# Operand loads, weight-sum stores, splits and norms of a feed-forward stage moved between queues and engines

## The chip, the cores and the metric

The kernel runs on one core of one Trainium2 chip. The metric is the device time of one launch in microseconds (us), the median of several runs. The core has five engines with an instruction queue each: TensorE (PE) multiplies matrices, VectorE (DVE) and GpSimd (POOL) work element by element, ScalarE (ACT) copies and evaluates functions, SyncE (SP) only issues DMAs. POOL and ACT can issue DMAs as well. Every queue is worked off in order.

## The reference

One layer of a diffusion backbone, on 128 context tokens and 2048 latent tokens of width 1024, all in float32:

```python
h = rmsnorm(x, norm1_g) * (1 + scale1) + shift1
z = h @ w_in                       # columns go to three groups A, B, C
mix = concat(A: gated linear attention, B: conv module, C: gMLP) @ w_out
x = x + gate1 * mix
h = rmsnorm(x, norm2_g) * (1 + scale2) + shift2
x = x + gate2 * (square(relu(h @ w_ff1)) @ w_ff2)      # 1024 -> 4096 -> 1024
y = rmsnorm(x, final_g)
```

Context and latent tokens have modulations of their own. The change touches the last four lines only.

## The kernel before, in words

Tokens stand in 17 tiles of 128 (tile 0 is the context). A float32 operand is split into a high part, rounded to the PE's float32r (ScalarE's copy), and a low part, the rest (a subtraction on DVE or POOL); each product is then three matmuls (mm3, L179): high x high, high x low, low x high. A "split" below is that copy and that subtraction.

The stages run one after another: attention, convolution and gating (to L1161), out_proj for tiles 16 down to 0 (L784, the loop at L1181), FF1 (loop at L1419), FF2 (loop at L1555). Both FF stages multiply 2 x 2 blocks by a Strassen-like scheme of seven products p = 0..6, whose operands are sums of blocks. The latent tokens make two groups g of 1024.

FF1: for each group, 16 iterations i over 256 columns of w_ff1. An iteration has 28 units on PE (seven products of four units, 12 matmuls a product), and in group 0 eight more for the context tile (ff1_context, L1307). Right operands (the tokens' sums, seven products of two halves) are made in out_proj (h2_pair, L835), stored to tb_d, and loaded and split by right_operand (L1173) once for a group: while out_proj and the first iteration run for group 0, and in the last iteration of group 0 for group 1. They lie in T tiles (18) and u tiles (12); the left operands, the weights, in v tiles (11), with left_operand (L1211) preparing the next iteration's in eight steps. `after(p)` (L1269) takes each product out of PSUM into fx, fy and fz, squares, combines and stores them to f_d as right operands of FF2.

FF2: eight chunks c of 512 hidden columns, four blocks b of four token tiles; a block has 28 units of three matmuls and two units of the context tile, 90 matmuls. Operands are loaded by w2_operand, f_operand and fc_operand into o tiles (24), T tiles and s tiles, and split in split_two (L1386), by DVE and POOL in turn. DVE adds each product to the output tiles ya (L1498); the residual x1 is loaded into these first (residual, L1465). The sums of w_ff2's blocks for chunk c + 1 are made in blocks 0 and 1 of chunk c by w2_prep (L1346): load, multiply by the gate and store three, then four combinations and store four, all on POOL. In the last chunk the tiles are normed (norm, L1477) and stored by SP.

What sets the order: `weave` (L154) puts a list of items (position, function) between PE's units, and PE's own instructions stay in program order. DMAs issued with ld_in_order (L136) stay in program order on SP's queue. The order of the rest on each engine is chosen when the kernel is built, by a planner that goes by its own costs; on the chip each queue then runs in that order. A tile of a pool with n buffers is written when the earlier one in its place was read for the last time.

Of the kernel before, what the change touches and what calls it, by code (L numbers as in the profile page):

```python
# [8 lines left out]
F32 = mybir.dt.float32  # L9
# [34 lines left out]
def tile_hybrid(  # L44
# [713 lines left out]

    staged = {}

# [23 lines left out]
    def out_proj(t):  # L784
# [9 lines left out]
        def done(half):  # L794
            def f(pz):
                fs = slice(half * 512, (half + 1) * 512)
                V.tensor_tensor(out=tmp[:, fs], in0=pz, in1=g1rows[cd][:, fs], op=ALU.mult)
                V.tensor_tensor(out=x1[:, fs], in0=tmp[:, fs], in1=x1[:, fs], op=ALU.add)
                if half == 1:
                    st.dma_start(out=x1_d[t], in_=x1)  # L800
                    ssq = const.tile([P, 1], F32, name="ssq3", bufs=2)
                    act(tmp, x1, AF.Square, accum_out=ssq)
                    rstd_of(ssq, ssq, D)
                    S.mul(tmp, x1, ssq)
            return f
# [367 lines left out]
    def right_operand(g, i, kk, dst):  # L1173

        unit = tunit if i < 4 else uunit
        hi, lo = unit(), unit()
        st.dma_start(out=lo.bitcast(F32).rearrange("p (k n) -> p k n", k=2), in_=tb_d[g][:, i, 2 * kk:2 * kk + 2])
        split_in_place(hi, lo, G if kk else V)
        dst[i, kk] = (hi, lo)
# [23 lines left out]
    def wunit(dt=F32R):  # L1203
        return fp.tile([P, D], dt, tag="v", name="v", bufs=11)

# [44 lines left out]
    def ff1_units(g, i, w, tb):  # L1250
# [4 lines left out]
        fx = xf.tile([P, 2, 512], F32, tag="fx", name="fx", bufs=2)  # L1255
        fy = xf.tile([P, 2, 512], F32, tag="fy", name="fy", bufs=1)
        fz = xf.tile([P, 3, 512], F32, tag="fz", name="fz", bufs=1)
# [11 lines left out]
        def after(p):  # L1269
            if p == 0:  # L1270
                S.copy(out=f00, in_=za)
            elif p == 1:
                V.tensor_tensor(out=f00, in0=f00, in1=gb, op=ALU.add)
                square(f00)
            elif p == 2:
                S.copy(out=f01, in_=za)  # L1276
            elif p == 3:
                S.copy(out=fy[:, 0], in_=zc)
            elif p == 4:
                V.tensor_tensor(out=f11, in0=fy[:, 0], in1=za, op=ALU.add)  # L1280
                square(f11)
            elif p == 5:
                V.tensor_tensor(out=f01, in0=f01, in1=zc, op=ALU.add)
                square(f01)
                comb(fz[:, 0], f00, f01, ALU.subtract)
                comb(fy[:, 1], f01, f11, ALU.add)
                comb(fy[:, 0], fy[:, 1], f00, ALU.subtract)
                st.dma_start(out=dst[:, 2:4], in_=fy)
            else:
                act(f10, za, AF.Relu)  # L1290
                V.tensor_tensor(out=f10, in0=f10, in1=f10, op=ALU.mult)
                comb(fz[:, 1], f10, fy[:, 0], ALU.subtract)
                st.dma_start(out=dst[:, 0:2], in_=fx)
                st.dma_start(out=dst[:, 4:7], in_=fz)
# [47 lines left out]
    for i, kk in ORDER[8:]:  # L1342
        right_operand(0, i, kk, TB[0])
    turn = None

    def w2_prep(i, unit, g2):  # L1346
# [10 lines left out]
        def gate():  # L1357
            for x in box:
                G.tensor_tensor(out=x, in0=x, in1=g2, op=ALU.mult)
            st.dma_start(out=d_[:, 0], in_=box[0][:, 0:512])  # L1360
            for f, p in ((0, 1), (1, 5)):
                st.dma_start(out=d_[:, p], in_=box[1][:, f * 512:f * 512 + 512])

        def step():
# [5 lines left out]
            for p, o in ((2, x), (4, y), (3, w), (6, z)):  # L1370
                st.dma_start(out=d_[:, p], in_=o)

# [12 lines left out]

    def split_two(hi, lo, src):  # L1386
        ctr[0] += 1
        S.copy(out=hi, in_=src)  # L1388
        (G if ctr[0] % 2 else V).tensor_tensor(out=lo, in0=src, in1=hi.bitcast(F32), op=ALU.subtract)  # L1389

    def operand(src, unit):

        hi, lo = unit(), unit()
        lv = lo.bitcast(F32)
        ld_in_order(out=lv.rearrange("p (a n) -> p a n", a=src.shape[1]), in_=src)
        split_two(hi, lo, lv)
        return hi, lo

    def w2_operand(c, p, out, unit=ounit):
        x = operand(w2_d[c][:, :, p], unit)  # L1400
        for q in range(CP):
            out[p, q] = [y[:, q * 512:(q + 1) * 512] for y in x]

    def f_operand(c, b, n, out, unit=ounit):
# [3 lines left out]
        s = f_d[c][g][:, ps, :, ts].rearrange("p a q n -> p (a q) n")  # L1408
        x = operand(s, unit if n < 3 else sunit)
        for a in range(s.shape[1]):  # L1410
            out[2 * n + a // 2, a % 2] = [y[:, a * 256:a * 256 + 256] for y in x]

    def fc_operand(c, out):
        x = operand(fc_d[c].rearrange("p q f n -> p (q f) n"), sunit)
        for q in range(2):
# [3 lines left out]
    for g in range(2):  # L1419
        for i in range(NP):  # L1420
            units = ff1_units(g, i, w, TB[g])
            items = []
            if g == 0:
                more, nxt_turn = ff1_context(i, w)
                units = units + more
                if turn is not None:
                    items.append((5, turn))
                turn = nxt_turn
            elif i == 0:
                items.append((5, turn))  # L1430
            if (g, i) == (0, 0):
                items += [(12, late3[0][1]), (20, late3[1][1])]
            if (g, i) != (1, NP - 1):
                w, steps = left_operand((i + 1) % NP)
                items += zip((0, 0.5, 5.5, 10.5, 13.5, 17.5, 18.5, 25.5), steps)
            if (g, i) == (1, NP - 1):

                items += [(x, lambda n=n: f_operand(0, 0, n, F, tunit)) for x, n in ((5, 0), (9, 1), (15, 2))]
                items.append((11, lambda: w2_operand(0, 0, w2, tunit)))
            if g == 1 and i == 3:  # L1440
# [18 lines left out]
    left, right = slice(0, 512), slice(512, 1024)  # L1459

    def tiles_of(b):

        return [NT - 1 - 8 * (b // 2) - 4 * (b % 2) - 2 * j for j in range(2)]

    def residual(b):  # L1465

        for t in sum([[e, e - 1] for e in tiles_of(b)], []):
            ya[t] = tunit(F32)
            ld_in_order(out=ya[t], in_=x1_d[t])

# [15 lines left out]
    def ff2_units(c, b, F, w2):  # L1486
# [19 lines left out]
        def unit(p, j, q):  # L1506
# [9 lines left out]
            if q == CP - 1:  # L1516
                after(p, j)

        return [lambda p=p, j=j, q=q: unit(p, j, q) for p in range(7) for j in range(2) for q in range(CP)]

# [3 lines left out]
    def context(c, b, Fc):  # L1524
# [3 lines left out]
        def load():  # L1528
# [3 lines left out]
            box.extend([ounit(), ounit()])  # L1532
            split_two(*box, rw)

# [13 lines left out]
    w2_operand(0, 1, w2)  # L1548
    residual(0)
    for p in range(2, 7):  # L1550
# [4 lines left out]
    for c in range(NC_):  # L1555
# [7 lines left out]
        for b in range(4):  # L1563
# [18 lines left out]
            if b == 0 and c > 0:  # L1582
                items += wl(c, (0.5, 5), (5, 6), w2)
            if c == 0 and b < 3:
                items.append((8, lambda: residual(b + 1)))
            if b in (0, 1) and more:
                items += zip((6, 12, 26), w2_prep(CP * (c + 1) + b, raw, g2r))
            weave(units, items)
# [34 lines left out]
```

## Time and profile before

| | us |
|---|---|
| runs | 2476.52, 2482.58, 2478.18 (median 2478.18) |
| profiled execution | 2481.85 |
| its span, first to last instruction | 2480.1 |

| engine | busy us | instructions |
|---|---|---|
| PE | 2270.2 | 12018 |
| DVE | 1818.1 | 2624 |
| ACT | 980.4 | 1788 |
| POOL | 1216.4 | 1087 |

The profiled execution is one run of the program with the hardware profiler on; its times are taken in us from the start of its span. A matmul's end is modelled, so a busy PE can still be slower than it could be. Where the profile names what ended an engine's idle time ("<-ACT v L176"), it is inferred from semaphores: the engine, the tile that it wrote, the line of the kernel.

### The profile page before, as it was taken

To read this page: it belongs to the slowest core of one execution; us is meant where nothing else is said; L and a number is where in the kernel's file an instruction comes from. 1 tells how busy PE (TensorE), PEld (TensorE's weight loads), DVE (VectorE), ACT (ScalarE), POOL (GpSimd) and SP (SyncE) were. 2 spreads that over 40 slices of the span, in tenths; PEclk is the share of its full clock that TensorE was granted. 3 is DMA by queue.
4 is the path that set the end of the run, shared out by engine and by line. 5 is a ranking of instruction groups with operands and counts; after the bars stand their busy time and mean duration, and the time that the engine had idled before them with its cause. 6 is when DMAs were issued, how large, how long until landed. Compare 5 with 4: busy or idle time off the path is not lost. (4 is left out here: it accounts for less than half of the span.)

```text
span 2480.1 us, 33032 instructions
## 1 busy us (share of the span) xinstructions
PE 2270.2 (92%) x12018; PEld 1852.5 (75%) x12018; DVE 1818.1 (73%) x2624; ACT 980.4 (40%) x1788; POOL 1216.4 (49%) x1087
## 2 busy tenths in 40 slices
PE   7999999999988987799999699899799999999996
PEld 5788886777767766588888477687587778778775
DVE  5887855877887865587777677776577777877577
ACT  4666664333344455333333332233332233233243
POOL 2332325444423445344334554644956866776742
PEclk9999999999989999899999799999899999999998
DMA  8655635333445456543444454545965666567564
GB/s 284 229 197 195 225 103 177 121 126 125 130 155 191 155 172 206 170 134 126 131 147 155 159 173 154 177 158 179 350 227 195 234 213 228 198 215 234 183 220 149
DMA packets 221764, 452.68 MB, mean 183 GB/s; under 512 B 17973, under 2 KB 118623, under 8 KB 218016
## 3 DMA queue, kind: packets, MB, share of 16 engines
q1 hardware_dynamic: 171456, 263.57, 32.4%
q0 software_dynamic: 50144, 186.99, 21.5%
q8 instruction: 95, 1.56, 0.3%
q14 instruction: 69, 0.57, 0.1%
HBM read 285.07 MB, written 165.43 MB: 182 GB/s over the span
## 5 line engine op out<-in xcount | busy, mean ns | idle before, releaser
L131 PE MATMUL z<-w,hb 128*128 128x512 f32 (+1 forms) x2486 | 558.4, 371 | 14.6 <-ACT hb L776 8.7
L131 PEld LDWEIGHTS z<-w,hb 128*128 128x128 f32 x2486 | 420.3, 191 | 90.5 <-ACT hb L776 8.9
L1388 ACT CAST o<-o 128x1024 fp32r<-128x1024 f32 x148 | 155.6, 1051 | 433.1 <-DMA o<-f_d 297.3
L131 PE MATMUL z<-T,v 128*128 128x512 f32 x1152 | 284.3, 400 | 33.0 <-ACT v L176 10.5
L131 PE MATMUL z<-u,v 128*128 128x512 f32 x1152 | 282.8, 404 | 31.9 <-ACT fy L1276 15.0
L131 PEld LDWEIGHTS z<-u,v 128*128 128x128 f32 x1152 | 223.2, 195 | 87.9 <-ACT fy L1276 20.3
L131 PE MATMUL z<-o 128*128 128x512 f32 x1080 | 265.4, 393 | 20.9 <-DVE T L1498 20.8
L131 PEld LDWEIGHTS z<-T,v 128*128 128x128 f32 x1152 | 220.1, 193 | 83.8 <-ACT v L176 10.7
L131 PE MATMUL g<-o 128*128 128x512 f32 x1116 | 269.6, 391 | 0.0
L131 PEld LDWEIGHTS z<-o 128*128 128x128 f32 x1080 | 201.2, 188 | 72.1 <-DVE T L1498 28.2
L1267 POOL TENSOR_TENSOR fz<-fx,fy 128x512 f32<-128x512 f32 x64 | 99.4, 1554 | 294.2 <-DVE fy L67 293.1
L131 PEld LDWEIGHTS g<-o 128*128 128x128 f32 x1116 | 210.6, 189 | 44.1
L1498 DVE TENSOR_TENSOR T<-T,z 128x512 f32<-128x512 f32 x256 | 171.7, 682 | 96.4 <-PE z L131 95.8
L67 DVE SCALAR_TENSOR_TENSOR cacc<-xp,wd,cacc 128x512 f32<-128x512 f32 (+2 forms) x360 | 237.5, 713 | 0.0
L1389 POOL TENSOR_TENSOR o<-o 128x1024 fp32r<-128x1024 f32 x71 | 177.1, 2503 | 120.3 <-ACT o L1388 119.9
L131 PE MATMUL z<-w,T 128*128 128x512 f32 x720 | 182.0, 407 | 7.0 <-ACT T L776 3.6
L1389 DVE TENSOR_TENSOR o<-o 128x1024 fp32r<-128x1024 f32 x77 | 159.9, 2078 | 26.0 <-ACT o L1388 17.8
L1498 DVE TENSOR_TENSOR T<-T,g 128x512 f32<-128x512 f32 x192 | 129.3, 683 | 67.3 <-PE g L131 66.8
L131 PE MATMUL z<-o,s 128*128 128x512 f32 x576 | 150.3, 405 | 23.2 <-DVE o L1389 19.7
L131 PEld LDWEIGHTS z<-w,T 128*128 128x128 f32 x720 | 137.0, 195 | 36.0 <-POOL T L777 4.5
L177 DVE TENSOR_TENSOR v<-raw,v 128x1024 fp32r<-128x1024 f32 x64 | 131.1, 2050 | 29.5 <-PE z L131 28.1
L131 PEld LDWEIGHTS z<-o,s 128*128 128x128 f32 x576 | 112.1, 196 | 50.6 <-DVE o L1389 22.2
(320 smaller groups left out, 3710.7 us busy)
## 6 DMA issues: line engine op xcount, KB each, us to landing
raw<-in_w_ff_dram SPq DMA_DIRECT2D x124, 512.0 KB
o<-f_d SPq DMA_DIRECT2D x93, 512.0 KB
o<-w_d SPq DMA_DIRECT2D x55, 512.0 KB
w_d<-raw POOLq DMA_DIRECT2D x98, 256.0 KB, 4.5
f_d<-fz POOLq DMA_DIRECT2D x32, 768.0 KB, 5.6
raw<-in_w_mod_dram SPq DMA_DIRECT2D x32, 512.0 KB
f_d<-fy POOLq DMA_DIRECT2D x32, 512.0 KB, 4.0
f_d<-fx POOLq DMA_DIRECT2D x32, 512.0 KB, 4.7
```

The source lines that it names most:

```text
L67: return V.scalar_tensor_tensor(out=out, in0=in0, scalar=scalar, in1=in1, op0=op0, op1=op1)
L131: tc.keep_in_program_order(T.matmul(out, lhsT, rhs, start=start, stop=stop, skip_group_check=read))
L177: order(V.tensor_tensor(out=lo, in0=src, in1=hi.bitcast(F32), op=ALU.subtract))
L1267: G.tensor_tensor(out=out, in0=a, in1=b, op=op)
L1388: S.copy(out=hi, in_=src)
L1389: (G if ctr[0] % 2 else V).tensor_tensor(out=lo, in0=src, in1=hi.bitcast(F32), op=ALU.subtract)
L1498: V.tensor_tensor(out=y, in0=y, in1=bank, op=ALU.add)
```

## The change

1. right_operand's loads are issued by SP in program order (they were POOL's).
2. The context tile's norm before FF1 is taken out of out_proj(0): it runs at unit 2.5 of FF1's first iteration, its scaling on DVE and not on ACT; the two halves that use it move from units 12 and 20 to 16 and 23.
3. In FF1 fy has two buffers and v tiles are 10; the sum f01 + f11 is DVE's (it was POOL's) and the two halves of fy change places, which f_operand undoes.
4. In group 0, from the second iteration on, the context units come first and the left operand's eight steps 8 units later.
5. w2_prep's stores are issued by ACT (they were POOL's). Its tiles in FF2 are T tiles (they were raw), and its items stand 4 units earlier.
6. split_two is told its engine: in chunk 0 all w2 splits are DVE's, later those of products 1, 3, 5, 6; of the f operands only the second (n = 1) is POOL's, except in the very first block; the context weights' are DVE's in blocks 0 and 1, POOL's in 2 and 3.
7. residual(0) and residual(1) are loaded in the last iteration of FF1 (units 19 and 25).
8. The last block of the last chunk runs all products of its first token pair and then those of the second.

```diff
@@ -756,7 +756,7 @@
-    staged = {}
+    staged, last_norm = {}, []
@@ -799,9 +799,17 @@
-                    act(tmp, x1, AF.Square, accum_out=ssq)
-                    rstd_of(ssq, ssq, D)
-                    S.mul(tmp, x1, ssq)
+                    def normed(scale):
+                        act(tmp, x1, AF.Square, accum_out=ssq)
+                        rstd_of(ssq, ssq, D)
+                        scale(tmp, x1, ssq)
+                    if t == 0:
+                        last_norm.append(lambda: normed(lambda o, i, m: V.tensor_scalar(o, i, m, None, op0=ALU.mult)))
+                    else:
+                        normed(S.mul)
@@ -1174,7 +1182,7 @@
-        st.dma_start(out=lo.bitcast(F32).rearrange("p (k n) -> p k n", k=2), in_=tb_d[g][:, i, 2 * kk:2 * kk + 2])
+        ld_in_order(out=lo.bitcast(F32).rearrange("p (k n) -> p k n", k=2), in_=tb_d[g][:, i, 2 * kk:2 * kk + 2])
@@ -1201,7 +1209,7 @@
-        return fp.tile([P, D], dt, tag="v", name="v", bufs=11)
+        return fp.tile([P, D], dt, tag="v", name="v", bufs=10)
@@ -1253,7 +1261,7 @@
-        fy = xf.tile([P, 2, 512], F32, tag="fy", name="fy", bufs=1)
+        fy = xf.tile([P, 2, 512], F32, tag="fy", name="fy", bufs=2)
@@ -1282,14 +1290,14 @@
+                V.tensor_tensor(out=fy[:, 0], in0=f01, in1=f11, op=ALU.add)
-                comb(fy[:, 1], f01, f11, ALU.add)
-                comb(fy[:, 0], fy[:, 1], f00, ALU.subtract)
+                comb(fy[:, 1], fy[:, 0], f00, ALU.subtract)
-                comb(fz[:, 1], f10, fy[:, 0], ALU.subtract)
+                comb(fz[:, 1], f10, fy[:, 1], ALU.subtract)
@@ -1341,6 +1349,16 @@
+    def tiles_of(b):
+        return [NT - 1 - 8 * (b // 2) - 4 * (b % 2) - 2 * j for j in range(2)]
+    def residual(b):
+        for t in sum([[e, e - 1] for e in tiles_of(b)], []):
+            ya[t] = tunit(F32)
+            ld_in_order(out=ya[t], in_=x1_d[t])
@@ -1357,9 +1375,9 @@
-            st.dma_start(out=d_[:, 0], in_=box[0][:, 0:512])
+            S.dma_start(out=d_[:, 0], in_=box[0][:, 0:512])
-                st.dma_start(out=d_[:, p], in_=box[1][:, f * 512:f * 512 + 512])
+                S.dma_start(out=d_[:, p], in_=box[1][:, f * 512:f * 512 + 512])
@@ -1368,7 +1386,7 @@
-                st.dma_start(out=d_[:, p], in_=o)
+                S.dma_start(out=d_[:, p], in_=o)
@@ -1383,21 +1401,20 @@
-    def split_two(hi, lo, src):
-        ctr[0] += 1
+    def split_two(hi, lo, src, eng):
-        (G if ctr[0] % 2 else V).tensor_tensor(out=lo, in0=src, in1=hi.bitcast(F32), op=ALU.subtract)
-    def operand(src, unit):
+        eng.tensor_tensor(out=lo, in0=src, in1=hi.bitcast(F32), op=ALU.subtract)
+    def operand(src, unit, eng):
-        split_two(hi, lo, lv)
+        split_two(hi, lo, lv, eng)
-        x = operand(w2_d[c][:, :, p], unit)
+        x = operand(w2_d[c][:, :, p], unit, V if c == 0 or p in (1, 3, 5, 6) else G)
@@ -1406,12 +1423,12 @@
-        x = operand(s, unit if n < 3 else sunit)
+        x = operand(s, unit if n < 3 else sunit, G if n == 1 and c + b else V)
-            out[2 * n + a // 2, a % 2] = [y[:, a * 256:a * 256 + 256] for y in x]
+            out[3 - a // 2 if n == 1 else 2 * n + a // 2, a % 2] = [y[:, a * 256:a * 256 + 256] for y in x]
-        x = operand(fc_d[c].rearrange("p q f n -> p (q f) n"), sunit)
+        x = operand(fc_d[c].rearrange("p q f n -> p (q f) n"), sunit, V)
@@ -1422,21 +1439,23 @@
-                units = units + more
+                units = more + units if i else units + more
-                    items.append((5, turn))
+                    items.append((8.5 if i else 5, turn))
-                items += [(12, late3[0][1]), (20, late3[1][1])]
+                items += [(2.5, last_norm[0]), (16, late3[0][1]), (23, late3[1][1])]
-                items += zip((0, 0.5, 5.5, 10.5, 13.5, 17.5, 18.5, 25.5), steps)
+                o_ = 8 if g == 0 and i else 0
+                items += [(x + o_, f) for x, f in zip((0, 0.5, 5.5, 10.5, 13.5, 17.5, 18.5, 25.5), steps)]
-                items.append((11, lambda: w2_operand(0, 0, w2, tunit)))
+                items += [(11, lambda: w2_operand(0, 0, w2, tunit)), (19, lambda: residual(0)), (25, lambda: residual(1))]
@@ -1457,16 +1476,6 @@
-    def tiles_of(b):
-        return [NT - 1 - 8 * (b // 2) - 4 * (b % 2) - 2 * j for j in range(2)]
-    def residual(b):
-        for t in sum([[e, e - 1] for e in tiles_of(b)], []):
-            ya[t] = tunit(F32)
-            ld_in_order(out=ya[t], in_=x1_d[t])
@@ -1516,6 +1525,8 @@
+        if last and b == 3:
+            return [lambda p=p, j=j, q=q: unit(p, j, q) for j in range(2) for p in range(7) for q in range(CP)]
@@ -1530,7 +1541,7 @@
-            split_two(*box, rw)
+            split_two(*box, rw, G if b > 1 else V)
@@ -1546,7 +1557,6 @@
-    residual(0)
@@ -1581,10 +1591,10 @@
-            if c == 0 and b < 3:
+            if c == 0 and 0 < b < 3:
-                items += zip((6, 12, 26), w2_prep(CP * (c + 1) + b, raw, g2r))
+                items += zip((2, 8, 22), w2_prep(CP * (c + 1) + b, lambda: tunit(F32), g2r))
```

## Rows read from the trace of the kernel before

**Rows 1.** The page's first part: busy us, share of the span, instructions.
```profile
PE 2270.2 (92%) x12018; PEld 1852.5 (75%) x12018; DVE 1818.1 (73%) x2624; ACT 980.4 (40%) x1788; POOL 1216.4 (49%) x1087
```

**Rows 2.** Stretches: us, PE PEld DVE ACT POOL busy, PE's granted clock, DMA share, GB/s.
```profile
979.50:1037.90 58.40, 32.27 (x122) 23.96 (x121) 36.21 (x38) 28.97 (x42) 27.99 (x25) 0.82 0.49 158
1037.90:1348.70 310.80, 310.80 (x1542) 263.32 (x1541) 238.71 (x225) 99.87 (x140) 127.77 (x109) 1.00 0.42 135
...
1375.40:1423.90 48.50, 28.57 (x88) 19.67 (x87) 34.37 (x28) 17.01 (x21) 29.52 (x22) 0.72 0.43 144
1423.90:1737.20 313.30, 296.19 (x1262) 240.20 (x1261) 235.10 (x215) 92.55 (x119) 164.07 (x134) 0.97 0.49 168
1737.20:1779.50 42.30, 26.07 (x92) 19.96 (x91) 19.66 (x19) 14.81 (x16) 38.17 (x29) 0.80 0.98 357
1779.50:2465.60 686.10, 649.93 (x2791) 526.37 (x2789) 512.00 (x596) 218.01 (x268) 442.04 (x284) 0.99 0.63 213
2465.60:2480.10 14.50, 0.01 (x1) 0.00 (x0) 7.12 (x17) 1.61 (x6) 2.17 (x4) 0.61 0.43 158
...
2444.90:2465.60 20.70, 20.70 (x90) 16.81 (x90) 19.30 (x38) 7.77 (x20) 2.65 (x5) 1.00 0.41 144
```

**Rows 3.** The switch of groups: loads on POOL, ACT's copy, landing times, DMA share.
```profile
1370.35 0.53 POOL L1177 DMA_DIRECT2D T<-tb_d  x1
...
1386.46 0.57 POOL L1177 DMA_DIRECT2D T<-tb_d  x1
...
1409.45 0.54 POOL L1177 DMA_DIRECT2D u<-tb_d  x1
...
1402.86 1.04 ACT L1170 CAST T<-T 128x1024 fp32r<-128x1024 f32 x1
...
DMA to landing us min/median/max: 3.9/6.1/9.1
...
1380.00:1385.00 5.00, 2.27 (x10) 1.50 (x8) 5.00 (x2) 0.90 (x2) 5.00 (x3) 1.00 0.00 0
```

**Rows 4.** FF2's splits by engine: ns min/median/max of one, first and last start.
```profile
L1389 DVE TENSOR_TENSOR o<-o x77: 1210/1366/5761, 1752.4 to 2443.0; 128x1024 fp32r<-128x1024 f32 x77
L1389 POOL TENSOR_TENSOR o<-o x71: 2359/2408/3374, 1744.2 to 2439.9; 128x1024 fp32r<-128x1024 f32 x71
```

**Rows 5.** FF1's start, timeline: start us, us, engine, [idle before it, ended by].
```profile
988.30 1.15 ACT L804 ACTIVATE raw<-w,ssq 128x1024 f32<-128x1024 f32 x1 [3.90 <-POOL ssq L166]
...
974.84 1.11 POOL L1177 DMA_DIRECT2D T<-tb_d  x2
...
1022.70 0.57 POOL L1177 DMA_DIRECT2D u<-tb_d  x1
...
990.44 5.04 PE L131 MATMUL z<-T,v 128*128 128x512 f32 x12 [10.46 <-ACT v L176]
...
1032.24 2.50 PE L131 MATMUL z<-u,v 128*128 128x512 f32 x5 [4.14 <-POOL u L1171]
```

**Rows 6.** PE's waits, 1425 to 1737: us in total, times, longest.
```profile
PE z L131 <- ACT fy L1276: 12.7, 4, 6.6
PE z L131 <- DVE fz L1280: 4.3, 2, 2.2
```

**Rows 7.** Stores of weight sums on POOL: ns min/median/max of one issue.
```profile
L1371 POOL DMA_DIRECT2D w_d<-raw x56: 542/560/569, 1766.5 to 2337.1; - x56
```

**Rows 8.** FF2's first block: PE's waits (1737 to 1780), SP's residual loads.
```profile
PE z L131 <- DVE o L1389: 9.8, 2, 8.3
PE g L131 <- POOL o L1389: 6.4, 1, 6.4
...
1730.12 2.08 SPq L137 DMA_DIRECT2D T<-x_d  x4
```

**Rows 9.** PE's waits in FF2 after that, 1779.5 to 2444.
```profile
PE z L131 <- DVE T L1498: 23.7, 19, 3.2
PE z L131 <- DVE o L1389: 11.4, 5, 2.3
```

**Rows 10.** ACT's waits, 1779 to 2440.
```profile
ACT o L1388 <- DMA o<-f_d: 283.1, 69, 17.1
```

## The prediction

> **What bounds the kernel now.** The page's first part comes first: TensorE (PE) is busy for 92% of the span, DVE for 73% [rows 1]. A busy PE is not a PE at its rate, so the stage table is next [rows 2]. The window 2444.9 to 2465.6 is one block of FF2 without a gap: 90 matmuls in 20.7 us, 0.23 us each. Fourteen iterations of group 0 of FF1 take 310.8 us, 22.2 each; an iteration of group 1 has 84 matmuls of the same kind, 84 x 0.23 = 19.3 us. Against these rates each stage has lost:
>
> - start of FF1: 58.4 - 22.2 = 36.2 us
> - switch to group 1: 48.5 - 19.3 = 29.2 us
> - the other 15 iterations of group 1: 313.3 - 15 x 19.3 = 23.8 us
> - first block of FF2: 42.3 - 20.7 = 21.6 us
> - the other 31 blocks: 686.1 - 31 x 20.7 = 44.4 us
> - after the last matmul: 14.5 us.
>
> That is 169.7 us in places where PE waits, part of it at the lower granted clock (the mean is 0.72 in the switch, so some of it ran at 1.2 GHz and not 2.4). Steady group 0 loses nothing (84 x 0.23 + 24 matmuls of half the width is 22.1). For each place the waits and timelines then say what ended last.
>
> **The change part by part.**
>
> *Right operands on SP's queue.* At the switch PE waits for splits of the operands just loaded. The loads sit in POOL's queue: one is issued at 1370.4, the next at 1386.5, the last at 1409.4, while one takes 3.9 to 9.1 us to land, and in 1380 to 1385 the DMA engines are idle (share 0.00) [rows 3]. So POOL's combinations and splits delay the issue. On SP nothing computes ahead of the loads. What is queued behind them there are two w_ff1 loads per iteration. A right operand's place is free when its product p is done, and it is wanted again one iteration later, 19.3 less 2.8 us of its own product. Landing (6.1) + ACT's copy (1.0) + split on POOL (2.4 [rows 4]) + a second load of the same product behind it (about 1.5) = 11 us; it fits into 16.5, but ACT, DVE and POOL have 14 copies and splits beside an iteration's own work, and the context product now stands ahead of the others and frees the places 2.9 us later. I leave 7 of the 29.2 us: gain **22**. Bounds: 8 (only 14 issues of 0.57 us leave POOL's queue) and 27 (2 us left).
>
> In a sentence of its own: the Trainium skill (DMA: Bandwidth & Descriptors, section "Issuing engines are not separate DMA queues") says that transfers started by any engine share the same 16 engines and that another issuing engine saves only issuing time, usually small. By that rule the gain here would be the lower bound, 8; the idle DMA engines in [rows 3] speak against it, since the issue itself is what comes late.
>
> *Start of FF1; last norm deferred.* PE's first wait is 10.46 us on ACT's copy of the weights. ACT had before it the context tile's scaling at 988.3, which had waited 3.9 us for POOL's power [rows 5]. The change takes this scaling out of ACT and runs it on DVE at unit 2.5; nobody wants it until unit 16. Then loads trickle, from 974.8 to 1022.7, and PE's last wait is for a split at 1032.2 [rows 5]. On SP they go when their places come free; those of products 4 to 6 lie in memory that out_proj's weights hold until about 979.5, product 3 waits for tiles of the last token pair. I expect PE to start about 4 us earlier and the iteration to end 12 us earlier on top: gain **16** of 36.2. Bounds 5 (half of the first wait) and 27 (the first wait and most of the later ones).
>
> *fy doubled, one combination on DVE, stores of weight sums off POOL.* In the rest of group 1 PE waits 12.7 us on ACT's copy into fy, which waits for fy's store, and 4.3 on DVE's fz [rows 6]. Two fy buffers end the first. Next is fz, one buffer as before, whose store goes from POOL with 3.9 us less ahead of it in two iterations (7 stores of 0.56 [rows 7]). DVE gets one add an iteration, at most the 1.21 us of a split of twice its size and a POOL pass of 2.4 before it [rows 4], and has room (235.1 of 313.3 us busy [rows 2]). The v pool falls from 11 to 10: 8 in use and 2 for the next; the third saved tile is only an earlier prefetch, hidden by an iteration. Gain **14** of 23.8 (12.7 and a little of the slow clock after it). Bounds 4 (fz takes fy's place) and 20.
>
> *First block of FF2.* PE waits 6.4 us for a split on POOL and 9.8 for two on DVE; SP puts four residual tiles between the weights' loads, at 1730.1 [rows 8]. Now the residuals are loaded before FF1 ends and all seven weight splits are DVE's: 1.21 us each where POOL isn't in the way, against 2.36 at least on POOL [rows 4]. Eight residual tiles are 4.2 MB ahead of the weights; at the 357 GB/s that this stage shows [rows 2] that is 11.7 us, from about 1728, when the places of product 3 are free, so the first weights may be some 2 us late. I leave 8.6 of 21.6: gain **13**. Bounds 4 and 18.
>
> *Other blocks of FF2.* PE waits 23.7 us for DVE's adds and 11.4 for DVE's splits [rows 9]. A chunk has 28 splits, so far 14 on each engine; now 19 on DVE. Its split is stretched by POOL's passes (minimum 1.21, median 1.37, maximum 5.76 us [rows 4]), so five more cost DVE 6.0 to 10 us in a chunk of 83, on an engine that is busy for 512.0 of 686.1 us [rows 2]; it rises to about 85%. Against this POOL loses 5 passes of 2.4 us and 14 issues of 0.56 (20 us a chunk with two preparations), and so stands in DVE's way less often. The sums' loads, moved from raw to T tiles and 4 units earlier, no longer hold the three raw buffers; they pass SP's queue ahead of the context load, which must wait when T is full. I set the sum at **0**, with -25 (one more late add of 0.8 us in each of 31 blocks) and +25 (most of the named waits gone).
>
> *Stores on ACT.* Cost to ACT: 7 issues a preparation, at POOL's 0.56 us [rows 7] about 4 us of a block's 20.7; below, next to nothing, above, 1 us each, 7 us. ACT is busy for 218.0 of 686.1 us [rows 2], and it idles 283.1 us before copies that wait for a load [rows 10]. Nothing is charged. Uncovered is the wait: a store stands in ACT's queue until POOL's sum is done, and behind it the copies of the next operands.
>
> *Last block by token pair.* The last four tiles' norms now spread. DVE is busy for 19.3 of 20.7 us in the last block and 7.1 after it [rows 2]. The same DVE work must be done, so only its gaps can go; and PE now waits for each add with one unit (1.4 us) between, not three. Gain **1**, bounds -4 and +5.
>
> Sum: 16 + 22 + 14 + 13 + 0 + 1 = 66 us. The profiled execution took 2481.85 us (span 2480.1), 3.7 above the median of the three runs. 2481.85 - 66 = 2415.9, less 3.7: **2412 us**.
>
> **The rivals.**
>
> *The transfers were the limit.* Then only the issuing time is saved: 8 at the switch, and at the start 9 (5 of the first wait, the rest of issues): 2412 + 14 + 7 = 2433. For it: the share is 0.98 in FF2's first block [rows 2]. Against: idle DMA engines at the switch.
>
> *DVE becomes FF2's bound.* Its 40 additional splits (5 in 8 chunks) each push an add that frees a bank: 40 x 1.21 = 48 us, so 2460. For it: 23.7 us of waits for these adds already, and 19.3 of 20.7 us busy in the last block. Against: 85% is not 100%, and POOL's shorter work shortens DVE's.
>
> *ACT's queue is blocked (slower than before).* 14 preparations in FF2 (56 stores, 4 in each second group) give 28 groups of stores. ACT can stand at each for two POOL passes, 2 x 2.4 = 4.8 us. With 1 us of slack PE loses 3.8 x 28 = 106: 2518. It decides from 2.6 us a group (28 x 2.6 = 73, 2485.6). For it: operands split on DVE come 2.3 us late already (11.4 in 5 waits [rows 9]). Against: ACT's 283.1 us of idling in the same stretch.
>
> **How the numbers follow.** Forecast 0.62, transfers 0.14, DVE 0.15, ACT 0.09. The forecast's own range is 2380 to 2444 (its terms' distances to their bounds, taken as independent, are about 32 either way). With rivals' tails, 8 in 10: 2372 to 2460. Within 0.3% (7.4 us) a measurement can't tell this kernel's time from no change. Faster: 0.62 + 0.14 + 0.12 of DVE's case; no change: the rest of DVE's and 0.02 of ACT's; slower 0.07.
>
> **What would show it.** Right: SP issues the right operands without POOL in between, the switch takes about 26 us and not 48.5; no wait on fy's store; PE's wait for POOL's split at FF2's start is gone; FF2's 31 blocks take 686 +- 25. Wrong: ACT idle before a store of sums with PE waiting for the copy behind it; waits for DVE's adds above 50 us in FF2; a wait of PE on a v tile in group 0.

## The result and the profile after

Forecast: faster, 2412 us. Measured: slower. The changed kernel takes 2514.1 us (median of 4 runs, 2508.99 to 2516.93) beside 2477.35 for the kernel before on the same chip: ratio 1.0145, 95% interval 1.0118 to 1.0172. Its profiled run took 2516.93 us.

The first part of the page after, for [rows 1]:

```profile
PE 2289.9 (91%) x12018; PEld 1865.1 (74%) x12018; DVE 1806.9 (72%) x2701; ACT 974.6 (39%) x1787; POOL 1032.2 (41%) x871
```

No engine but PE is busier: DVE and ACT are about as busy as before, POOL 184 us less. What grew is PE's waiting. The stages, for [rows 2] (same columns):

```profile
973.40:1021.90 48.50, 31.38 (x124) 24.05 (x123) 41.28 (x40) 24.76 (x38) 25.12 (x17) 0.79 0.56 190
...
1332.30:1361.40 29.10, 25.61 (x112) 20.71 (x111) 19.58 (x19) 11.73 (x16) 12.11 (x9) 0.88 0.64 230
1361.40:1410.40 49.00, 29.69 (x88) 20.66 (x87) 32.09 (x26) 15.57 (x19) 25.44 (x15) 0.68 0.40 148
1410.40:1725.30 314.90, 295.05 (x1262) 240.65 (x1261) 231.85 (x232) 93.26 (x120) 134.04 (x101) 0.97 0.51 171
1725.30:1765.80 40.50, 25.54 (x91) 18.89 (x89) 28.31 (x24) 13.58 (x15) 23.25 (x14) 0.79 0.90 325
1765.80:2507.00 741.20, 671.10 (x2791) 538.50 (x2790) 508.61 (x642) 218.51 (x272) 335.48 (x159) 0.96 0.58 199
2476.20:2507.00 30.80, 24.82 (x91) 18.50 (x90) 23.61 (x50) 9.88 (x27) 6.30 (x8) 0.89 0.38 137
2507.00:2515.20 8.20, 0.00 (x0) 0.00 (x0) 3.84 (x9) 0.72 (x2) 1.10 (x2) 0.64 0.34 128
```

Every stage begins where PE's last matmul of the one before ends, so the differences add up:

| stage | before | after | forecast gain | measured gain |
|---|---|---|---|---|
| up to the end of FF1's first iteration | 1037.9 | 1021.9 | 16 | 16.0 |
| group 0's next 14 iterations | 310.8 | 310.4 | 0 | 0.4 |
| switch (last iteration of group 0, first of group 1) | 75.2 | 78.1 | 22 | -2.9 |
| rest of group 1 | 313.3 | 314.9 | 14 | -1.6 |
| FF2's first block | 42.3 | 40.5 | 13 | 1.8 |
| FF2's other 31 blocks | 686.1 | 741.2 | 0, with the last block 1 | -55.1 |
| after the last matmul | 14.5 | 8.2 | in the 1 above | 6.3 |
| together, the spans 2480.1 and 2515.2 | | | 66 | -35.1 |

In the 31 blocks PE idles 741.2 - 671.1 = 70.1 us, for 36.2 before; the other 21 us are PE itself, at a mean granted clock of 0.96 and not 0.99. One wait shows how the two belong together. Three stretches: a wait of PE, the 3.41 us after it, and what follows.

```profile
2130.48:2134.06 3.58, 0.00 (x0) 0.00 (x0) 3.53 (x3) 0.00 (x0) 3.27 (x3) 0.96 0.74 253
2134.06:2137.47 3.41, 3.41 (x9) 2.69 (x10) 0.00 (x0) 0.65 (x1) 2.31 (x2) 0.54 0.99 306
2137.47:2141.00 3.53, 3.53 (x17) 2.90 (x16) 2.65 (x2) 2.82 (x4) 2.10 (x1) 1.00 1.08 401
```

After it PE runs 3.4 us near its lower level (granted 0.54; the levels are 1.2 and 2.4 GHz), 9 matmuls where [rows 2] have 15 (3.41 / 0.23). So this wait cost some 6 x 0.23 = 1.4 us beyond itself.

What PE waited for, first in FF2 between its first and its last block (for [rows 9]), then in group 1 after the switch (for [rows 6]); us in total, times, longest:

```profile
PE z L131 <- DVE T L1507: 36.1, 21, 4.7
PE z L131 <- DVE o L1406: 26.4, 7, 4.5
...
PE z L131 <- ACT fx L1279: 13.7, 2, 7.2
PE z L131 <- DVE fz L1288: 4.4, 6, 2.3
PE z L131 <- ACT fy L1284: 1.7, 1, 1.7
```

The wait on fy's store is gone, as forecast (12.7 to 1.7), and two waits on ACT's copy into fx cost 13.7. In FF2 both kinds of waits grew. The seven on DVE's o are one in the first block of each chunk but chunk 0. Here is the one of chunk 4 (timeline; PE's and DVE's adds left out):

```profile
2122.77 5.63 POOL L1377 TENSOR_TENSOR T<-T,cacc 128x1024 f32<-128x1024 f32 x2 [1.13 <-DMA T<-in_w_ff_dram]
...
2125.62 0.33 ACTq L1378 DMA_DIRECT2D w_d<-T  x1
...
2127.79 1.69 DVE L1406 TENSOR_TENSOR o<-o 128x1024 fp32r<-128x1024 f32 x1
...
2128.42 0.33 ACTq L1380 DMA_DIRECT2D w_d<-T  x1
...
2128.87 1.06 ACT L1405 CAST o<-raw 128x1024 fp32r<-128x1024 f32 x1 [6.31 <-PE g L131]
...
2130.59 1.21 DVE L1406 TENSOR_TENSOR o<-o 128x1024 fp32r<-128x1024 f32 x1
...
2131.73 2.28 DVE L1406 TENSOR_TENSOR o<-raw,o 128x1024 fp32r<-128x1024 f32 x1
...
2134.06 0.80 PE L131 MATMUL z<-o,s 128*128 128x512 f32 x1 [3.58 <-DVE o L1406]
```

Read from below: PE waits for the context weights' split (o<-raw,o), which the change gave to DVE in this block. On DVE it stands behind two other splits. Its copy on ACT came late too: ACT stood at two stores of sums (ACTq) until POOL's passes of 2.8 us each were done (the profile names PE's g for the end of ACT's idle time; the second store was issued 0.45 us before the copy began). So the trace offers two causes in one place, and rival 3 (ACT's queue blocked, 2518) seemed to have it all. Chunk 7 already speaks against it: no sums are made there, the copy is done at 2410.97, and PE still waits 3.96 us for the split, which DVE begins at 2415.85 behind two others. The experiments show how much each cause is worth.

### The profile page after: what moved, and what is told of

Its sections match the earlier page's. It is cut to its first block, busy times and chain, and to the rows that moved or that the text cites. A ratio compares the mean times of both kernels' runs of the same rounds, so it can differ in the third digit from the quotient of the medians.

```text
span 2515.2 us, 32992 instructions
## 1 busy us (share of the span) xinstructions
PE 2289.9 (91%) x12018; PEld 1865.1 (74%) x12018; DVE 1806.9 (72%) x2701; ACT 974.6 (39%) x1787; POOL 1032.2 (41%) x871
## 5 line engine op out<-in xcount | busy, mean ns | idle before, releaser
L131 PE MATMUL z<-T,v 128*128 128x512 f32 x1152 | 287.0, 401 | 30.1 <-ACT fx L1279 13.7
L131 PE MATMUL z<-o 128*128 128x512 f32 x1080 | 277.3, 406 | 37.5 <-DVE T L1507 37.4
L131 PEld LDWEIGHTS z<-o 128*128 128x128 f32 x1080 | 208.7, 196 | 94.2 <-DVE T L1507 49.1
L131 PEld LDWEIGHTS z<-T,v 128*128 128x128 f32 x1152 | 220.5, 194 | 78.3 <-ACT fx L1279 14.5
L1275 POOL TENSOR_TENSOR fz<-fx,fy 128x512 f32<-128x512 f32 x64 | 119.1, 1861 | 356.3 <-DVE fy L67 330.3
L1406 POOL TENSOR_TENSOR o<-o 128x1024 fp32r<-128x1024 f32 x52 | 130.3, 2507 | 230.3 <-ACT o L1405 224.8
L131 PE MATMUL z<-o,s 128*128 128x512 f32 x576 | 153.0, 410 | 40.5 <-DVE o L1406 29.1
L131 PEld LDWEIGHTS z<-o,s 128*128 128x128 f32 x576 | 112.3, 197 | 69.5 <-DVE o L1406 32.5
L177 DVE TENSOR_TENSOR v<-cacc,v 128x1024 fp32r<-128x1024 f32 x64 | 79.8, 1247 | 114.4 <-ACT v L176 114.4
L1406 DVE TENSOR_TENSOR o<-o 128x1024 fp32r<-128x1024 f32 x96 | 148.4, 1547 | 9.1 <-ACT o L1405 8.8
## 6 DMA issues: line engine op xcount, KB each, us to landing
raw<-in_w_ff_dram SPq DMA_DIRECT2D x96, 512.0 KB
o<-f_d SPq DMA_DIRECT2D x93, 512.0 KB
o<-w_d SPq DMA_DIRECT2D x55, 512.0 KB
raw<-in_w_mod_dram SPq DMA_DIRECT2D x32, 512.0 KB
f_d<-fy POOLq DMA_DIRECT2D x32, 512.0 KB, 4.0
f_d<-fx POOLq DMA_DIRECT2D x32, 512.0 KB, 3.6
```

The lines of the kernel that those rows point to most:

```text
L131: tc.keep_in_program_order(T.matmul(out, lhsT, rhs, start=start, stop=stop, skip_group_check=read))
L177: order(V.tensor_tensor(out=lo, in0=src, in1=hi.bitcast(F32), op=ALU.subtract))
L1275: G.tensor_tensor(out=out, in0=a, in1=b, op=op)
L1406: eng.tensor_tensor(out=lo, in0=src, in1=hi.bitcast(F32), op=ALU.subtract)
```

## The experiments

Each number is a median; in brackets stands the interval of its ratio to the kernel before, measured on the same chip (2477 to 2483 us there). "31 blocks" is FF2 from the end of its first block to the last matmul, in the profiled run: 686.1 before, 741.2 after. A profiled run can lie 12 us from its kernel's median (2478.6 and 2490.3 below), so small differences between these figures say little.

**One edit alone, or one undone.** In the changed kernel, the stores on POOL again; in the kernel before, only the stores on ACT:

```
-            S.dma_start(out=d_[:, 0], ...)     # and the other two lines
+            st.dma_start(out=d_[:, 0], ...)
```

> The changed kernel (2514 us) with one edit undone: the stores of the weight sums are POOL's again; splits, places and times stay as changed. ACT theory (a store on ACT waits in its queue until POOL has made the sum, and the copies of the next operands wait behind it): FF1's two 7 us waits on the copy into fx go with the slow clock after them (about 20 us) and FF2's stretch of 777 us falls by 40 to 50: 2445 to 2455. DVE theory (19 of 28 splits on DVE make it late): only FF1's 20 us come back: 2490 to 2500. Timing theory (the sums' loads and passes, 4 units earlier, collide with the context operand): also 2490 to 2500.

2528.6 us (1.0149 to 1.0221), 31 blocks 745.1. Nothing comes back: in chunk 4 the copy of the context weights is now done at 2127.8, but their split stands at the same place in DVE's queue and starts at 2133.3, and in FF1 a wait on fz (22.2 us in 5) takes the place of that on fx.

> The kernel before (2478 us) with one edit: the stores of the weight sums are issued by ACT. ACT theory: about 20 us more in FF1 (second group, iterations 4 and 8) and 20 to 40 more in FF2: 2515 to 2540. DVE and timing theories: FF2 doesn't change, FF1 loses at most 20: 2478 to 2498.

2461.8 us (0.9899 to 0.9947): **faster** than before, 31 blocks 679.0. All three theories missed this one; the forecast's third rival, as priced, falls with these two runs. In the profiled runs 12.9 of the 21.3 us gained lie where the stores are (5.8 in group 1, 7.1 in the 31 blocks).

Splits by the engines in turn again, and the sums' steps at their old units:

```
+        ctr[0] += 1
-        eng.tensor_tensor(out=lo, ...)
+        (G if ctr[0] % 2 else V).tensor_tensor(out=lo, ...)
```

> The changed kernel (2514 us) with split_two's engines in turn again (14 of 28 splits in a chunk on DVE, not 19; the context weights' in turn). DVE theory: the 40 us of FF2 come back: 2470 to 2480. ACT theory: the context copy is held by the stores all the same, within 10 us of 2514; POOL's splits lengthen what the stores wait for, so rather above than below.

2486.3 us (0.9990 to 1.0033), 31 blocks 712.2: 29 of the 55 come back.

```
-                items += zip((2, 8, 22), w2_prep(...))
+                items += zip((6, 12, 26), w2_prep(...))
```

> The changed kernel (2514 us) with the sums' steps in FF2 at units 6, 12 and 26 again (were 2, 8 and 22). Timing theory: the context operand at unit 3 is free of them, its 29 us of waits on PE and the slow clock after them (8 x 3.4) go: 2465 to 2480. ACT theory: the stores hold ACT's queue as long as before and other copies stand behind them: 2500 to 2525.

2497.9 us (1.0041 to 1.0094), 31 blocks 723.5: 18 come back. The wait on the context split stays (33.3 us in 7), and its rows show why. Chunk 4 again:

```profile
2113.14 1.05 ACT L1405 CAST o<-raw 128x1024 fp32r<-128x1024 f32 x1 [0.22 <-DMA raw<-in_w_ff_dram]
...
2117.92 1.40 DVE L1406 TENSOR_TENSOR o<-o 128x1024 fp32r<-128x1024 f32 x1
...
2120.64 1.99 DVE L1406 TENSOR_TENSOR o<-o 128x1024 fp32r<-128x1024 f32 x1
...
2122.55 2.28 DVE L1406 TENSOR_TENSOR o<-raw,o 128x1024 fp32r<-128x1024 f32 x1
...
2124.89 1.65 PE L131 MATMUL z<-o,s 128*128 128x512 f32 x3 [4.67 <-DVE o L1406]
```

Now the copy is done at 2114.2, no store ahead of it, and the split still starts at 2122.55, third in DVE's row. It is the place in DVE's queue that decides.

**Both together**, the two edits above in one kernel:

> The changed kernel (2514 us) with both put back: splits by the engines in turn (alone 2486) and the sums' steps at units 6, 12 and 26 (alone 2498). Overload theory (in a chunk's first block DVE gets more splits than it can do before unit 16, beside POOL's passes over the sums; either edit takes a part of the load away): the two add up, 28 + 16, 2465 to 2475. One-wait theory (both edits free the same wait, the context operand's): no better than the better of the two, 2480 to 2490.

2457.1 us (0.9890 to 0.9930), 31 blocks 685.1, as before the change; PE no longer waits for an o tile of DVE. They more than add up (56 for 29 + 18): each alone leaves the context operand late, behind POOL's passes and ACT's stores of them (23.3 us of waits on POOL's split in the first) or behind DVE's splits. The ACT stores are still in.

**Which split?** The context's split alone, and with the sums' times:

```
-            split_two(*box, rw, G if b > 1 else V)
+            split_two(*box, rw, G)
```

> The changed kernel (2514 us); the context weights' split is POOL's in all four blocks (it was DVE's in blocks 0 and 1). Overload theory, with the context operand as the one that suffers: PE's waits on it (26.4 us in 7) go with most of the slow clock after each, 2470 to 2490. Exchange theory (POOL is as late there as DVE, behind the passes over the sums): 2505 to 2525.

2490.3 us (1.0017 to 1.0052), 31 blocks 708.5 (in a profiled run of 2478.6, the fastest of ten); the wait moves to POOL's split (27.0 us in 8), while those on DVE's adds fall to 17.3. The median lies just above the range of the overload theory.

> The changed kernel (2514 us) with the context weights' split on POOL in all blocks (alone 2490) and the sums' steps at units 6, 12 and 26 (alone 2498); the other splits keep their engines. Context theory (the whole loss in FF2 is the context operand, late behind two splits in DVE's queue or behind two passes in POOL's, and either edit alone leaves the other): PE's 26 us of waits on it and the slow clock go, 2452 to 2465, like alternation and times together (2457). Load theory (17 splits in a chunk on DVE still make its adds late): 2475 to 2490.

2495.0 us (1.0045 to 1.0095), 31 blocks 731.4. The context theory falls: PE's wait on the operand is gone, and in its place stand waits of up to 9 us for DVE's adds. The load theory's range is missed too, by 5 us. PE's waits between the first and the last block, then the longest in the timeline:

```profile
PE z L131 <- DVE T L1507: 60.7, 17, 9.0
...
1957.26 1.34 DVE L1406 TENSOR_TENSOR o<-o 128x1024 fp32r<-128x1024 f32 x1 [5.65 <-ACT o L1405]
...
1961.43 0.81 ACTq L1389 DMA_DIRECT2D w_d<-T  x2
1962.36 1.04 ACT L1405 CAST o<-o 128x1024 fp32r<-128x1024 f32 x1 [4.67 <-POOL T L1386]
...
1963.49 1.23 DVE L1406 TENSOR_TENSOR o<-o 128x1024 fp32r<-128x1024 f32 x1 [2.02 <-issue]
...
1964.63 1.28 DVE L1507 TENSOR_TENSOR T<-T,z 128x512 f32<-128x512 f32 x2
1965.37 1.22 PE L131 MATMUL z<-o 128*128 128x512 f32 x2 [9.04 <-DVE T L1507]
```

POOL's last sum, ACT's store of it, ACT's copy of the next operand, DVE's split, DVE's add, PE: a chain through four queues. Here DVE stands at splits, 5.65 us before the first and 2.02 before the second, and adds whose products are ready stand behind them. Of PE's 9.04 us DVE is idle for about 3; the rest it spends on splits and adds that came late. With engines in turn the same copy on ACT came as late, but the split behind it was POOL's, DVE went on adding, and PE waited 2.64 us:

```profile
1960.80 4.74 POOL L1407 TENSOR_TENSOR o<-o 128x1024 fp32r<-128x1024 f32 x2
1960.83 1.27 DVE L1508 TENSOR_TENSOR T<-T,z 128x512 f32<-128x512 f32 x2
...
1961.56 3.01 PE L131 MATMUL z<-o 128*128 128x512 f32 x12 [2.64 <-DVE T L1508]
1961.80 1.05 ACT L1406 CAST o<-o 128x1024 fp32r<-128x1024 f32 x1 [2.93 <-POOL T L1386]
```

Three kernels test this, all from the last one. The stores on POOL; two splits of the first block to POOL; and only the split behind the held copy to POOL:

> The run with the context's split on POOL and the sums at units 6, 12 and 26 (2495 us, with PE waiting 55.6 us in 16 for DVE's adds), and the stores of the sums on POOL again. Chain theory (POOL's pass, ACT's store behind it, ACT's copy behind the store, DVE's split behind the copy, DVE's add behind the split, PE): with ACT free the waits of 6 to 9 us are gone, 2460 to 2475. Load theory (17 splits in a chunk are too many for DVE, whoever stores): 2490 to 2505.

2492.5 us (1.0026 to 1.0055), 31 blocks 722.3. No better in time. The chain is gone (DVE stands 12.1 us at copies into o, not 33.9; PE's waits for adds fall to 35.2 us, one of them still 7.8), but POOL's issues come back (fz 20.3 us in 4 in FF1), DVE's splits take up to 4.6 us beside POOL's passes, and PE waits 10.9 us for them. This run alone would speak for load.

```
-    ... V if c == 0 or p in (1, 3, 5, 6) else G
+    ... V if c == 0 or p in (1, 3, 6) else G
-    ... G if n == 1 and c + b else V
+    ... G if (n == 1 or (n, b) == (2, 1)) and c + b else V
```

> The run with the context's split on POOL and the sums at units 6, 12 and 26 (2495 us), and two more splits of a chunk's first block on POOL (w2's product 5 and the third f operand: in this block 3 of 7 on DVE, not 5; in the chunk 15, not 17; the other blocks as they were). Bunching theory (DVE stands in the first block's splits, and its adds of the next block with it; the count of a chunk doesn't matter): the waits of 6 to 9 us at the start of block 1 go, 2455 to 2468. Count theory (each split on DVE beyond 14 costs its share): 2480 to 2490.

2494.4 us (1.0040 to 1.0075), 31 blocks 728.2: both expectations miss. Two splits less for DVE in a chunk changed nothing, so it isn't the count. (The six long waits stand at the start of a chunk's third block, b = 2, in this run and the last one, not of block 1: the two splits moved were not the ones ahead of them.)

```
-    ... G if n == 1 and c + b else V
+    ... G if (n == 1 or (n, b) == (0, 3)) and c + b else V
```

> The run with the context's split on POOL and the sums at units 6, 12 and 26 (2495 us), and one split more of a chunk on POOL: the first f operand loaded in block 2, whose copy on ACT stands behind the last stores of the sums of block 1. Chain theory (DVE idles for that copy with the adds of block 2 behind it, 6 to 9 us in each of six chunks): these six waits shrink to 2 to 3 us, as with splits in turn, and with the slow clock after them 30 to 45 us come back: 2450 to 2465. Load theory: one split less of 17 changes the time by under 10 us: 2485 to 2495.

2470.4 us (0.9958 to 0.9989), 31 blocks 708.1. One split, 25 us: the chain, if less than expected. The six waits of 6.6 to 9.0 us are now 3.6 to 4.8, not 2 to 3; an earlier link, the split that waits for the copy before, is still DVE's. PE's waits on adds:

```profile
PE z L131 <- DVE T L1507: 38.6, 15, 4.8
```

**The other stages.** w_ff1's loads in SP's program order; the last block product by product; fy single (its sum on POOL):

```
-            ld.dma_start(out=rw[r]..., in_=w_ff1...)
+            ld_in_order(out=rw[r]..., in_=w_ff1...)
```

> The changed kernel (2514 us); the loads of w_ff1 are put into SP's program order, so the right operands' loads at the switch stand before the load that SP waits 25.4 us for. SP-order theory (the switch gained nothing since that one load held SP's queue): the last iteration of group 0 and the first of group 1, 78.1 us together, fall to 56 to 65: 2494 to 2503. Places theory (the places in T and u come free too late, and ACT's copies and the splits are the limit): 74 to 80 us, 2508 to 2520.

2510.3 us (1.0108 to 1.0139); the switch takes 69.6 us, not 78.1. Between the two: SP's order was 8.5 us of it, and the switch is now 5.6 us shorter than the 75.2 before the change. PE's waits that are left are for splits (POOL's u 6.4, DVE's u 4.8) and for fz (4.6).

```
-        if last and b == 3:
-            return [... for j in range(2) for p in range(7) for q in range(CP)]
```

> The changed kernel (2514 us); the last block runs product by product again. Bank theory (by token pair each product's unit comes back to the bank that DVE has just to add from, so PE waits): the last block falls from 30.8 to 21 to 23 us and what follows it grows from 8.2 to 12 to 15: 2508 to 2512. Split theory (the last block loses its time to late splits, not to the order): the block stays at 28 to 31 and the rest grows: 2518 to 2523.

2514.2 us (1.0129 to 1.0165): no change in time. The parts move about as the bank theory says: in the profiled runs the last block with what follows takes 23.6 + 12.8 us, by token pair 30.8 + 8.2.

> The changed kernel (2514 us) with fy in one buffer, its sum on POOL and its halves as before. Theory of exchange (the second buffer took 12.7 us of waits away, and fx's 13.7 behind the sums' passes took their place): FF1's second group within 5 us of the changed kernel's, 2509 to 2519. Theory that it gained and the stores took it back: with fy single both waits stand, 2524 to 2530.

2522.0 us (1.0149 to 1.0195), between the expectations; group 1 after the switch takes 315.9 us, by the second buffer 314.9. An exchange there; the rest of the difference lies outside these iterations.

**Putting it together.** The kernel with splits in turn and late sums, once with the stores on POOL, once with the two edits on order above (w_ff1's loads, the last block), and that one with fy single:

> Splits in turn and sums at units 6, 12 and 26 (2457 us), and the stores of the sums on POOL again. Store theory (7 issues of 0.56 us on POOL in each of 16 preparations cost more than ACT's standing behind the sums): 2470 to 2480, as in the kernel before, where they were worth 18 to 21. ACT theory (ACT's queue held by the stores is what is left of the loss): 2435 to 2450.

2474.6 us (0.9961 to 1.0003), 17.5 more than with the stores on ACT: near the 21.6 that the kernel before gained (2483.3 to 2461.8 on one chip). What these stores are worth depends on the order around them: in the changed kernel it was 14.5 by the medians, with intervals that overlap, and in the run at 2495 us nothing (2492.5 with POOL's).

> The changed kernel with four edits: splits in turn, sums at units 6, 12 and 26 (these two 2457), the loads of w_ff1 in program order (switch 69.6 us, not 78.1) and the last block product by product (36.4 us with its tail, not 39.0). If the four don't touch each other, 2457 - 8.5 - 2.6 = 2446; if the switch's gain only moves a wait into the next iterations, 2455.

**2445.4 us** (0.9836 to 0.9885), the fastest here, 1.4% under the kernel before; 31 blocks 680.2, switch 69.7. It is the time expected if the four edits don't touch each other.

> The best version so far (2445 us) with fy in one buffer, its sum on POOL and its halves as before. Exchange theory (as in the changed kernel, where a single fy gave 2522 for 2514): 2445 to 2453. Order theory (in FF1's iterations 4 and 8 the stores on ACT alone gave 84.3 us, with the second fy 94.9 and more; a single fy lets the sums pass earlier): 2430 to 2440.

2462.5 us (0.9892 to 0.9939): worse, against both expectations. In the profiled runs group 1 is about the same (314.5 for 317.2: iterations 4, 5, 8 and 9 gain 16, the others lose 13); the switch and FF2's first block lose 4 each. The profiled run took 2452.5 us, so some 10 of the 17 us stand in no trace and stay open.

## Why the prediction was wrong, by its steps

**Start of FF1** (16): measured 16.0, in part by luck. The first wait of PE is 6.0 us for the copy of the weights where it was 10.46 [rows 5], and the stage falls from 58.4 to 48.5 us, 9.9 less. The other 6.1 us lie ahead of it: the stage begins that much earlier, which no run ties to the change. PE's last instruction of out_proj ends anywhere from 966.1 to 976.3 in the changed kernel and the 15 made from it, at 980.0 before and at 974.8 with only the stores on ACT.

**Switch** (22): -2.9, the step failed. "On SP nothing computes ahead of the loads" was true and not enough. SP's queue at the switch:

```profile
1337.26 1.15 SPq L137 DMA_DIRECT2D T<-tb_d  x2
...
1341.02 3.40 SPq L137 DMA_DIRECT2D T<-tb_d  x5
1369.90 0.38 SPq L1225 DMA_DIRECT2D raw<-in_w_ff_dram  x1
1370.38 0.51 SPq L137 DMA_DIRECT2D T<-tb_d  x1
1371.07 0.57 SPq L137 DMA_DIRECT2D u<-tb_d  x1
...
1374.59 3.23 SPq L137 DMA_DIRECT2D u<-tb_d  x5
...
SPq L1225 <- DVE cacc L1244: 25.4, 1, 25.4
```

Seven right operands are issued by 1344.4; then SP stands 25.4 us at a w_ff1 load whose place DVE's sums still hold, and the other seven stand behind it. In the kernel before SP stood as long at the same load, with nothing of the switch behind it:

```profile
SPq L1217 <- DVE cacc L1236: 26.5, 1, 26.5
```

The prediction named these loads, put them behind the operands and never asked when their places come free. With the order mended 8.5 us come back, and the switch is 5.6 us shorter than before the change, less than the lower bound of 8. Most of the 22 was not the issue but the splits. In that run ACT's last copy of an operand ends at 1381.2, and PE's last wait for a split only at 1398.75; the splits stand in DVE's and POOL's queues behind adds and combinations that wait for PE's own products:

```profile
1376.37 4.84 ACT L1178 CAST u<-u 128x1024 fp32r<-128x1024 f32 x5
...
1398.75 2.50 PE L131 MATMUL z<-u,v 128*128 128x512 f32 x5 [4.43 <-POOL u L1179]
```

By the Trainium skill's rule weighed in the forecast (DMA: Bandwidth & Descriptors, "Issuing engines are not separate DMA queues": another issuing engine saves only issuing time) 8 was the answer here; the 5.6 of this run agree with it, not with 22. For the stores the issuing time was not small in sum: 112 issues of 0.56 us on POOL are 63 us of its queue, and 17.5 to 21.6 us of the kernel's time in two of the orders tried.

**fy and group 1** (14): -1.6. The wait on fy went as forecast, but PE then waits for fx: in iterations 4 and 8 ACT stands 15.3 and 16.2 us at the stores of the w_ff2 sums made there, its copies behind it.

```profile
1477.64 1.04 ACT L176 CAST v<-cacc 128x1024 fp32r<-128x1024 f32 x1 [15.28 <-POOL T L1387]
...
1481.80 1.22 PE L131 MATMUL z<-T,v 128*128 128x512 f32 x2 [6.51 <-ACT fx L1279]
```

With the stores on POOL it is fz that PE waits for, 22.2 us. In both, POOL's sums stand ahead of its combinations; that these alone set the end isn't shown.

**FF2's first block** (13): 1.8. Residuals and weights came as forecast: PE's wait of 6.4 on POOL [rows 8] went, those of 9.8 on DVE fell to 3.8. In their place is one of 9.8 us on ACT's copy of the context weights, which stands behind the sums' stores.

**FF2's other blocks** (0): -55.1, twice the lower bound of -25. This step turned the forecast. It priced five more splits on DVE by their duration and found room, since DVE is busy for three quarters. Room there was, and the price of 6 to 10 us a chunk never came: DVE didn't rise to 85%, it is busy for 508.6 us where it was 512.0, and between the first and the last block its 140 splits take 202 us where 104 took 209. Wrong was that room on average is what counts. DVE's queue runs in order, and the adds that free PE's banks (the places it writes products to), like the context weights' split, stand in it behind other splits. In PE's 28 waits for DVE (62.5 us, the first two lines of waits above) DVE is busy for all but 0.3 us, 47 of them with splits; its idle time lies elsewhere, where it waits for PE's products. At the start of block 1 of chunk 2:

```profile
1952.17 5.67 POOL L1377 TENSOR_TENSOR T<-T,cacc 128x1024 f32<-128x1024 f32 x2 [1.96 <-DMA T<-in_w_ff_dram]
...
1953.61 2.04 DVE L1406 TENSOR_TENSOR o<-o 128x1024 fp32r<-128x1024 f32 x1
...
1955.56 2.83 DVE L1406 TENSOR_TENSOR s<-s 128x512 fp32r<-128x512 f32 x1
...
1958.31 1.27 DVE L1507 TENSOR_TENSOR T<-T,z 128x512 f32<-128x512 f32 x2
1959.04 1.53 PE L131 MATMUL z<-o 128*128 128x512 f32 x4 [3.55 <-DVE T L1507]
```

Beside POOL's pass over the sums, 4 units earlier by the change, the two splits take 2.04 and 2.83 us (1.21 and 0.68 at the least), and both adds stand behind them. With the sums at their old units DVE spends 7.8 us of PE's waits for adds on splits, not 23.2; the wait for the context split stays. That fits the experiments: the two edits together bring the 55 us back, each alone only a part.

The chain of the run at 2495 us (DVE idle at a split, adds behind it) is shown by the 25 us of one split, but for that kernel: in the changed kernel DVE stands at copies into o for 8.2 us in all:

```profile
DVE o L1406 <- ACT o L1405: 8.2, 15, 1.2
```

With engines in turn and late sums (2457 us) it stands there for 58.1 us, while PE waits only 32.2 for adds. (The Trainium skill, PSUM — Partial Sum Buffer, "Engine vs sequencer instructions", calls these queues strictly first in, first out; the rows with two ready adds behind a split agree.)

**Stores on ACT** (0): a gain of 17.5 to 21.6 in two orders and of none in a third, which neither the sum nor a rival had. The rival's mechanism is real (ACT idle before a store, PE waiting for the copy behind it, as the prediction said it would look) but shows as time of PE where the split behind the copy is DVE's, or where PE waits for the copy itself (fx, and the 9.8 us above). That its 2518 lies near the 2514 measured is chance: with the stores on POOL again nothing came back. The second rival (DVE the bound, 2460) had the right engine and almost the right loss in FF2, 48. Its reason holds in part: splits do hold back the adds, but not each by its duration. In the run at 2495 us two splits less changed nothing, and another one gave 25 us.

**Last block** (1): -9.4 in the block and +6.3 after it, together -3.1, within the bounds of -4 and +5.

Open: between the kernel with one split moved (708.1 in the 31 blocks) and splits in turn (685.1) lie 23 us. The last block accounts for 6 (32.5 and 26.6); the rest wasn't taken apart. Nor was the last step of load against chain: with stores on POOL the fixed engines lose about as much as with ACT by the chain, with DVE's splits at 1.79 us in the mean and not 1.48. That POOL's passes stretch DVE's splits is read from rows; no run tested it alone.

## What to carry to other kernels

Before an instruction is moved to another engine, list what stands behind it in that engine's queue and what it will wait for: its cost there is the wait that it passes on, not its duration, and a busy share of three quarters says nothing about it. The same holds for a DMA moved to SP: look at when the place of every load ahead of it comes free. When a trace shows two causes for one wait, undo each alone and both together; here the two edits that mattered gave about half or less alone, and the likelier-looking third, the stores on ACT, was a gain or nothing.

## What the runs showed of the hardware

A store's issue takes 0.33 us on ACT (ACTq rows above) where it took 0.56 on POOL [rows 7]. Beside it stands what the issue holds: up to 16.2 us of ACT's queue, which no row of the store itself shows, only the idle time of the instruction after it.
